# Higher scheduling priority for the chain from the output projection to the first MLP input tiles, and row scalings on VectorE, in a decoder layer on one core

## The chip, the core and the metric

The kernel runs on one core of a Trainium2 chip. TensorE (PE) does the matrix products and the transposes, VectorE (DVE) and ScalarE (ACT) work on rows of 128 partitions, GpSimd (POOL) does a few small operations, SyncE (SP) issues the transfers between the memory of the chip and the core's SBUF. PSUM holds what TensorE writes. The metric is the device time of one execution in microseconds (us); the median of the runs counts.

## The reference

One decoder layer over 2048 tokens of width 1024, in float32. A conditioning vector gives six vectors (shift, scale and gate of each half of the layer), and every half normalises its input rows first:

```
mod = silu(c) @ w_ada + b_ada
sh1, sc1, ga1, sh2, sc2, ga2 = split(mod, 6)
h   = rms_norm(x, g_attn) * (1 + sc1) + sh1
z   = h @ w_in                      # both attention groups, one product
mix = concat(sliding_window(z), forgetting(z)) @ w_out
x   = x + ga1 * mix
h2  = rms_norm(x, g_mlp) * (1 + sc2) + sh2
u   = causal_conv3(h2 @ w_up)       # 2 * 2816 columns
a, g = split(u, 2)
x   = x + ga2 * ((silu(g) * a) @ w_down)
y   = rms_norm(x, g_final)
```

`rms_norm` multiplies each row by 1/sqrt(mean of its squares + eps). The sliding-window group looks at 128 keys, the forgetting group at all earlier ones, so its work grows with the position.

## The kernel before

The 2048 tokens are cut into four blocks of 512, each in four tiles of 128 rows (t0 to t3) by two halves of 512 columns. Every float32 product is made of three TensorE products of a high part and a low part: ScalarE casts the high part (`hh`, `wh`, `ph`, `yh`), VectorE subtracts it from the whole (`hl`, `wl`, `pl`, `yl`).

A block goes through three stages. s1 normalises its rows, transposes them and multiplies by `w_in`. s2 is the attention, here mostly that of the forgetting group: scores `s` in PSUM, bias on ScalarE into `t` (L973), running maximum `mx` and the sum `acc` on VectorE, the maximum subtracted (L1002, L1006), exponential on ScalarE (L1007), split into `ph` and `pl` (L716, L717), product with the values into `o` (L1051, L1054); small transposes (`mt`, `lt`, `mb`) carry the row maxima and sums. s3 is the output projection (L1171), the rest of the layer's first half, and the MLP (its up-projection is L1289). In time: s1 of block 0; s1 of blocks 1 and 2 beside the attention of block 0; then s3 of block 0 beside the attention of block 1, s3 of block 1 with s1 of block 3 beside the attention of block 2, s3 of block 2 beside the attention of block 3, and s3 of block 3 alone. The two streams of a stage are merged in the order in which the program is written.

The place that the change touches lies in s3 between the output projection and the up-projection; each block passes it once. For each tile t and each half of the columns: VectorE multiplies the projection `d` by the gate into `gtmp` (L1245) and adds it to the residual row `x1row` (L1247); SP stores the row (L1248); ScalarE squares it and sums the squares into `ss` (`sumsq`, L487). After the second half: POOL makes `rs` = (sum + eps)^-0.5 in two instructions (L491, L492), and ScalarE scales the first half of the row in place (`pscale`, L114) and the second half into `gtmp` (L1255). Then `lazy_h` makes the input tiles of the MLP one by one, in two parts of 256 tokens (t0 and t1, then t2 and t3): TensorE transposes 128x128 pieces of the scaled rows into `d` (L513), ScalarE applies scale and shift (`hraw`, L521, with `scl` and `mod`) and casts `hh` (L114), VectorE subtracts `hl` (L526). The first block's own rows go the same way at the very start (`prep_tile`, rows `xrow`, tiles `xt`, first product L278), beside the first part of `mod` (L201 and L203 on VectorE, summed over partitions by L258 on TensorE, finished by L263 to L265).

What sets the order: a tile scheduler takes the whole program, keeps a priority for each instruction (by default the order in which it was written) and writes a fixed order for each engine; at run time an engine takes its instructions in that order and waits at the head of its queue. VectorE's and SP's order at the start is written out by hand, and is kept.

## Time and profile before

| | |
|---|---|
| median of 3 runs | 2670.57 us (2666.57 to 2671.02) |
| the profiled execution | 2663.14 us, its span 2661.4 us, mean granted TensorE clock 0.976 of full |
| TensorE busy | 2544.1 us, 96% of the span |
| VectorE, ScalarE, GpSimd busy | 1918.8 us (72%), 1472.0 us (55%), 91.7 us (3%) |

The profiled execution lies 7.43 us under the median of the timed runs. Busy time of TensorE contains matmuls whose ends are modelled, so what matters is where it has no work at all, and the stretches in which its clock is below full.

### The profile page before, as it was taken

To read this page: it belongs to the slowest core of one execution; us is meant where nothing else is said; L and a number is where in the kernel's file an instruction comes from. 1 tells how busy PE (TensorE), PEld (TensorE's weight loads), DVE (VectorE), ACT (ScalarE), POOL (GpSimd) and SP (SyncE) were. 2 spreads that over 40 slices of the span, in tenths; PEclk is the share of its full clock that TensorE was granted. 3 is DMA by queue.
4 is the path that set the end of the run, shared out by engine and by line. 5 is a ranking of instruction groups with operands and counts; after the bars stand their busy time and mean duration, and the time that the engine had idled before them with its cause. 6 is when DMAs were issued, how large, how long until landed. Compare 5 with 4: busy or idle time off the path is not lost.

```text
span 2661.4 us, 38402 instructions
## 1 busy us (share of the span) xinstructions
PE 2544.1 (96%) x12852; PEld 2155.2 (81%) x12852; DVE 1918.8 (72%) x3813; ACT 1472.0 (55%) x3085; POOL 91.7 (3%) x171
## 2 busy tenths in 40 slices
PE   7999989799999999989999999799998999999998
PEld 5888888688887889878888888688877878888887
DVE  5568767799998668778888767888888876344433
ACT  4456665655667675575556665755555665421222
POOL 1001000100000010010000000100000000000000
PEclk9999999799999999999999999899998999999999
DMA  6967679576557876756666799365554577655564
GB/s 229 303 204 256 194 226 339 179 257 212 183 188 216 284 253 213 254 184 234 227 231 235 256 304 315 100 216 193 185 168 142 173 238 236 227 197 191 190 236 175
DMA packets 304769, 588.24 MB, mean 221 GB/s; under 512 B 32188, under 2 KB 137396, under 8 KB 304572
## 3 DMA queue, kind: packets, MB, share of 16 engines
q1 hardware_dynamic: 304572, 585.79, 65.8%
q8 instruction: 102, 1.67, 0.3%
q14 instruction: 95, 0.78, 0.1%
HBM read 440.95 MB, written 144.71 MB: 220 GB/s over the span
## 4 chain that ended last, share of the span: by engine, by line
PE 83%; DVE 5%; DMA 5%; ACT 4%; issue 2%; POOL 1%; SPq 1%; POOLq 0%; DVEq 0%; ACTq 0%
PE d L1289 36%; PE d L1171 21%; PE d L611 8%; PE s L956 4%; PE d L639 3%; PE o L1054 2%; PE o L1051 2%; PE d L278 1%; PE mb L988 1%; DVE t L1002 1%; PE s L786 1%; DMA yraw<-yd 1%; DMA q<-qd 1%; DMA wada<-in_w_ada_dram 1%; PE pt L828 1%
## 5 line engine op out<-in xcount | busy, mean ns | idle before, releaser
L1289 PE MATMUL d<-hh,wkh 128*128 128x512 f32 (+1 forms) x920 | 352.9, 386 | 13.4 <-DVE halo L1333 8.7
L1289 PE MATMUL d<-hl,wkh 128*128 128x512 f32 (+1 forms) x920 | 353.7, 386 | 0.0
L1289 PE MATMUL d<-hh,wkl 128*128 128x512 f32 (+1 forms) x920 | 352.5, 384 | 0.0
L381 DVE TENSOR_TENSOR wl<-wr,wh 128x1024 fp32r<-128x1024 f32 (+5 forms) x184 | 218.9, 1190 | 84.1 <-ACT wh L380 82.1
L973 ACT ACTIVATE t<-s,bc 128x256 f32<-128x256 f32 (+3 forms) x464 | 201.1, 483 | 135.7 <-PE s L956 72.0
L380 ACT CAST wh<-wr 128x1024 fp32r<-128x1024 f32 (+5 forms) x184 | 188.7, 1026 | 152.0 <-PE d L1289 62.8
L1319 ACT ACTIVATE u<-d,cb,cw 128x512 f32<-128x512 f32 x176 | 136.3, 777 | 207.7 <-PE d L1289 190.8
L716 ACT CAST ph<-t 128x512 fp32r<-128x512 f32 (+2 forms) x304 | 176.8, 590 | 119.3 <-PE o L1051 117.8
L1322 DVE SCALAR_TENSOR_TENSOR u<-d,cw,u 128x511 f32<-128x511 f32 x176 | 130.4, 743 | 150.7 <-ACT u L1319 149.6
L717 DVE TENSOR_TENSOR pl<-t,ph 128x512 fp32r<-128x512 f32 (+2 forms) x304 | 192.5, 644 | 31.5 <-ACT ph L716 31.2
L1289 PE MATMUL d<-hl,wh 128*128 128x512 f32 (+1 forms) x552 | 211.9, 385 | 0.0
L1289 PE MATMUL d<-hh,wh 128*128 128x512 f32 (+1 forms) x552 | 211.2, 384 | 0.4 <-ACT hh L114 0.4
L1289 PEld LDWEIGHTS d<-hh,wkh 128*128 128x128 f32 x920 | 173.9, 190 | 46.5 <-DVE halo L1333 9.3
L1289 PE MATMUL d<-hh,wl 128*128 128x512 f32 (+1 forms) x552 | 210.9, 383 | 0.0
L956 PE MATMUL s<-q,kkb 128*128 128x256 f32 (+2 forms) x1024 | 195.1, 309 | 7.3 <-ACT t L973 3.1
L1289 PEld LDWEIGHTS d<-hh,wkl 128*128 128x128 f32 x920 | 174.9, 190 | 32.0
L1289 PEld LDWEIGHTS d<-hl,wkh 128*128 128x128 f32 x920 | 174.9, 190 | 31.3 <-DVE hl L526 0.2
L1007 ACT ACTIVATE t<-t 128x512 f32<-128x512 f32 (+2 forms) x304 | 170.2, 601 | 13.0 <-DVE t L1006 10.1
L956 PEld LDWEIGHTS s<-q,kkb 128*128 128x128 f32 x1024 | 152.0, 194 | 19.9 <-ACT t L973 5.3
L1051 PE MATMUL o<-ph,vvb 128*128 128x256 f32 (+2 forms) x512 | 150.8, 310 | 10.0 <-ACT ph L716 3.6
L1054 PE MATMUL o<-pl,vvb 128*128 128x256 f32 (+2 forms) x512 | 146.7, 306 | 8.7 <-DVE pl L717 8.7
L611 PE MATMUL d<-hh,wh 128*128 128x512 f32 x360 | 142.0, 398 | 5.5 <-DVE lf L654 3.9
(232 smaller groups left out, 6078.9 us busy)
## 6 DMA issues: line engine op xcount, KB each, us to landing
wkh<-wsu SPq DMA_DIRECT2D x110, 512.0 KB, 3.3
wkl<-wsu SPq DMA_DIRECT2D x110, 512.0 KB, 4.2
wr<-in_w_up_dram SPq DMA_DIRECT2D x66, 512.0 KB, 4.8
wkh<-wsd SPq DMA_DIRECT2D x55, 512.0 KB, 3.9
wkl<-wsd SPq DMA_DIRECT2D x55, 512.0 KB, 4.3
wada<-in_w_ada_dram SPq DMA_DIRECT2D x96, 256.0 KB, 5.5
wr<-in_w_in_c_dram SPq DMA_DIRECT2D x45, 512.0 KB, 4.3
wsu<-wh SPq DMA_DIRECT2D x44, 512.0 KB, 2.9
```

The costliest lines, as they stand in the source:

```text
L380: nc.scalar.copy(wh, raw)
L381: nc.vector.tensor_sub(wl, raw, r32(wh))
L611: nc.tensor.matmul(ps, a[:, k, :], b[k], start=(k == 0 and i == 0), stop=(k == KT - 1 and i == 2),)
L716: nc.scalar.copy(ph[:, e0:], src[:, e0:])
L717: nc.vector.tensor_sub(pl[:, e0:], src[:, e0:], r32(ph[:, e0:]))
L956: nc.tensor.matmul(ps[:, o + low(c0) : o + w], st["kks"][kb // 4][:, (kb % 4) * P : (kb % 4 + 1) * P], qs[a][:, low(c0) : w], start=(a == ...
L973: nc.scalar.activation(tt[:, plain : o + w], ps[:, plain : o + w], AF.Identity, bias=bias(kb))
L1007: nc.scalar.activation(t1, t1, AF.Exp)
L1051: nc.tensor.matmul(po[:, c:], v, ph[:, o + c : o + w], start=(kb == 0), stop=False)
L1054: nc.tensor.matmul(po[:, c:], v, pl[:, o + c : o + w], start=False, stop=(kb == nkb - 1))
L1171: nc.tensor.matmul(acc[t], l[:, ts], r[:, k % 2, :], start=(i == 0 and l is ah and r is wh), stop=(i == n_k - 1 and l is al),)
L1289: nc.tensor.matmul(ps[:, c], w[a][:, k, :], b[k][:, c], start=(k == 0 and i == 0), stop=(k == KT - 1 and i == 2),)
```

## The change

A scheduling context `first()` raises the priority of what is written inside it by 400 places. It is put around the second half's loop over the four tiles (gate, add, sums, `rsqrt`, scalings) and around the making of the MLP's input tiles (`lazy_h` with two parts). Inside the loop the scaling of the first half of a row goes from ScalarE to VectorE, and the store of the row is written behind the sums. At the start the eight scalings of the first block's rows go from ScalarE to VectorE. 24 instructions change their engine in all (8 at the start, 4 for each block). Lines behind the new function are 4 further down than before, those behind the loop 8 further.

```diff
+AHEAD = 400
...
+    def first():
+        return tc.high_priority(offset=AHEAD)
...
                 j = made[part]
-                a, b = h_pair(hh, hl, j)
-                ps = side_ps(w) if side else dense_ps(w)
-                transposes(ps, rows[part * nt : (part + 1) * nt], j)
-                modulate_one(a[:, c], b[:, c], ps, j, a0, s0)
+                with first() if parts == 2 else nullcontext():
+                    a, b = h_pair(hh, hl, j)
+                    ps = side_ps(w) if side else dense_ps(w)
+                    transposes(ps, rows[part * nt : (part + 1) * nt], j)
+                    modulate_one(a[:, c], b[:, c], ps, j, a0, s0)
...
         rs = rms(row)
         for r in row:
-            pscale(r, r, rs)
+            if n == 0:
+                nc.vector.tensor_scalar(r, r, rs, None, ALU.mult)
+            else:
+                pscale(r, r, rs)
...
-                tmp = tp.tile([P, 512], F32, tag="t", name="gtmp")
-                row = rows[t][half]
-                nc.vector.tensor_mul(tmp, r[t], gb)
-                adder = nc.vector
-                adder.tensor_add(row, row, tmp)
-                nc.sync.dma_start(x1_d[n][t * P : (t + 1) * P, cs], row)
-                if half == 0:
-                    sss.append(sums())
-                sumsq(row, sss[t][:, half : half + 1], tmp)
-                if half == 1:
-                    rs = rsqrt(sss[t])
-                    pscale(rows[t][0], rows[t][0], rs)
-                    nc.scalar.activation(tmp, row, AF.Copy, scale=rs)
-                    rows[t][1] = tmp
+                with first() if half == 1 else nullcontext():
+                    tmp = tp.tile([P, 512], F32, tag="t", name="gtmp")
+                    row = rows[t][half]
+                    nc.vector.tensor_mul(tmp, r[t], gb)
+                    nc.vector.tensor_add(row, row, tmp)
+                    if half == 0:
+                        sss.append(sums())
+                    sumsq(row, sss[t][:, half : half + 1], tmp)
+                    nc.sync.dma_start(x1_d[n][t * P : (t + 1) * P, cs], row)
+                    if half == 1:
+                        rs = rsqrt(sss[t])
+                        nc.vector.tensor_scalar(rows[t][0], rows[t][0], rs, None, ALU.mult)
+                        nc.scalar.activation(tmp, row, AF.Copy, scale=rs)
+                        rows[t][1] = tmp
```

What the scheduler makes of it shows in the orders of the engines. The orders before and after agree outside the start, the four places between projection and up-projection, and one long stretch: from block 2's place on, through the attention of block 3, nearly every engine's order is another one. POOL's order is unchanged, SP's changes in a few rows.

VectorE in block 1, beside the attention, before. L1247 are the adds of t2 and t3, L1002 the subtraction of the maximum, L1032 and L1036 the reciprocal `rl` of the attention's sums:

```order
L1247 TENSOR_TENSOR x1row<-x1row,gtmp 128x512
L1002 TENSOR_TENSOR t<-t,mm 128x512 x6
L933 TENSOR_TENSOR mx<-t 128x512
L378 TENSOR_TENSOR wl<-wr,wh 128x512
L1245 TENSOR_TENSOR gtmp<-d,gb_12125 128x512
L378 TENSOR_TENSOR wl<-wr,wh 128x512
L1032 TENSOR_REDUCE rl<-lt 128x2
L1014 TENSOR_TENSOR acc<-t 128x512
L1247 TENSOR_TENSOR x1row<-x1row,gtmp 128x512
L939 TENSOR_TENSOR mx<-mx,t 128x512
L1036 RECIPROCAL rl<-rl 128x2
```

The same place of the changed kernel, from the add of t2 on:

```order
L1255 TENSOR_TENSOR x1row<-x1row,gtmp 128x512
L1010 TENSOR_TENSOR t<-t,mm 128x512 x6
L1262 TENSOR_SCALAR x1row<-x1row,rs 128x512
L941 TENSOR_TENSOR mx<-t 128x512
L382 TENSOR_TENSOR wl<-wr,wh 128x512
L1254 TENSOR_TENSOR gtmp<-d,gb_12125 128x512
L382 TENSOR_TENSOR wl<-wr,wh 128x512
L1040 TENSOR_REDUCE rl<-lt 128x2
L1262 TENSOR_SCALAR x1row<-x1row,rs 128x512
L1022 TENSOR_TENSOR acc<-t 128x512
L947 TENSOR_TENSOR mx<-mx,t 128x512
L1255 TENSOR_TENSOR x1row<-x1row,gtmp 128x512
```

The six subtractions still stand ahead of t3's gate and add; two scalings (of t1 and t2) have come in between, and t0's stands a few rows ahead of the first row shown.

TensorE in block 2, beside the attention, before. L956 are scores, L1051 and L1054 products with the values, L513 the transposes of the scaled rows:

```order
L988 MATMUL mb<-ident,rl 128x128 x2
L956 MATMUL s<-q,kkb 128x256 x4
L1051 MATMUL o<-ph,vvb 128x256
L513 MATMUL d<-ident,x1row 128x128 x3
L1054 MATMUL o<-pl,vvb 128x256
L1051 MATMUL o<-ph,vvb 128x256
```

In the changed kernel the same `mb` products and four score products are followed by L1059 and L1062, six of each in turn, and then:

```order
L1059 MATMUL o<-ph,vvb 128x256
L1062 MATMUL o<-pl,vvb 128x256
L964 MATMUL s<-q,kkb 128x256 x8
L517 MATMUL d<-ident,x1row 128x128 x6
L964 MATMUL s<-q,kkb 128x256 x4
```

Eleven value products and eight score products that stood behind the first transposes now stand ahead of them, and the six transposes of the first part stand together.

ScalarE in block 3, with no attention beside it, before. L487 are the sums of squares (the first row holds four of the first half of the columns and that of t0), L114 on `x1row` and L1255 the two scalings of a row, L521 and L114 on `hraw` the input tiles:

```order
L487 ACTIVATE gtmp,ss<-x1row 128x512 x5
L114 ACTIVATE x1row<-x1row,rs 128x512
L1255 ACTIVATE gtmp<-x1row,rs 128x512
L487 ACTIVATE gtmp,ss<-x1row 128x512 x2
L114 ACTIVATE x1row<-x1row,rs 128x512
L1255 ACTIVATE gtmp<-x1row,rs 128x512
L114 ACTIVATE x1row<-x1row,rs 128x512
L1255 ACTIVATE gtmp<-x1row,rs 128x512
L521 ACTIVATE hraw<-d,mod,scl 128x256 x3
L487 ACTIVATE gtmp,ss<-x1row 128x512
L114 ACTIVATE hh<-hraw 128x256 x3
```

And in the changed kernel:

```order
L491 ACTIVATE gtmp,ss<-x1row 128x512 x5
L1263 ACTIVATE gtmp<-x1row,rs 128x512
L491 ACTIVATE gtmp,ss<-x1row 128x512
L1263 ACTIVATE gtmp<-x1row,rs 128x512
L491 ACTIVATE gtmp,ss<-x1row 128x512
L525 ACTIVATE hraw<-d,mod,scl 128x256 x3
L115 ACTIVATE hh<-hraw 128x256
L491 ACTIVATE gtmp,ss<-x1row 128x512
L1263 ACTIVATE gtmp<-x1row,rs 128x512
```

The first three `hraw` stand behind the scaling of t1 and no longer behind the scalings of t2, and the scalings of `x1row` are gone from ScalarE.

## Rows read from the trace of the kernel before

**Rows 1.** TensorE's waits: for which line, us in total, times, longest.

```profile
PE d L513 <- ACT x1row L114: 14.5, 4, 7.6
PE sd L513 <- ACT xrow L114: 10.0, 4, 6.3
```

**Rows 2.** Stretches: busy time by engine, granted clock (PEclk), DMA share.

```profile
0.00:30.00 30.00, 12.80 (x49) 10.33 (x50) 14.35 (x31) 21.65 (x42) 6.82 (x19) 1.00 0.92 330
...
1133.00:1180.00 47.00, 38.51 (x243) 34.60 (x242) 39.64 (x79) 40.92 (x96) 11.33 (x10) 0.89 0.49 158
1660.00:1720.00 60.00, 45.26 (x292) 39.92 (x291) 47.97 (x91) 46.41 (x109) 7.99 (x10) 0.89 0.32 104
1720.00:2240.00 520.00, 495.01 (x2589) 420.35 (x2588) 424.73 (x883) 310.44 (x699) 2.46 (x12) 0.97 0.56 187
2274.00:2310.00 36.00, 31.60 (x189) 28.70 (x188) 13.51 (x27) 22.61 (x50) 3.64 (x8) 0.91 0.39 139
```

**Rows 3.** Durations of two forms: ns min/median/max, first and last start.

```profile
L114 ACT ACTIVATE x1row<-x1row,rs x16: 704/722/735, 478.1 to 2288.1; 128x512 f32<-128x512 f32 x16
L201 DVE TENSOR_SCALAR acc<-wada,cc x12: 457/482/487, 11.8 to 570.5; 128x512 f32<-128x512 f32 x12
```

**Rows 4.** Timeline of the start: start us, length us, instruction, idle before.

```profile
16.03 1.34 ACT L114 ACTIVATE xrow<-xrow,rs 128x512 f32<-128x512 f32 x2 [0.83 <-POOL rs L492]
...
12.46 5.47 DVE L203 SCALAR_TENSOR_TENSOR acc<-wada,cc,acc 128x512 f32<-128x512 f32 x7 [0.19 <-DMA wada<-in_w_ada_dram]
20.82 1.23 DVE L381 TENSOR_TENSOR wl<-wr,wh 128x1024 fp32r<-128x1024 f32 x1 [2.89 <-ACT wh L380]
...
25.32 0.16 DVE L265 SCALAR_TENSOR_TENSOR scl<-mod,gat 128x2 f32<-128x2 f32 x1
...
27.67 2.08 PE L278 MATMUL d<-hh,wh 128*128 128x512 f32 x4 [4.54 <-ACT hh L114]
```

**Rows 5.** Timeline of block 0's place.

```profile
507.75 1.22 PE L956 MATMUL s<-q,kkb 128*128 128x512 f32 x2 [2.99 <-DVE mod L215]
```

**Rows 6.** Timeline of block 1's place.

```profile
1148.42 0.15 DVE L1036 RECIPROCAL rl<-rl 128x2 f32<-128x2 f32 x1
...
1152.67 0.63 ACT L487 ACTIVATE gtmp<-x1row 128x512 f32<-128x512 f32 x1
...
1148.72 0.40 PE L988 MATMUL mb<-ident,rl 128*128 128x128 f32 x2 [3.83 <-DVE rl L1036]
...
1161.58 1.14 PE L513 MATMUL d<-ident,gtmp 128*128 128x128 f32 x4 [3.21 <-ACT hraw L521]
...
1153.49 5.57 POOL L491 TENSOR_SCALAR rs<-ss 128x1 f32<-128x1 f32 x1 [2.47 <-ACT gtmp L487]
1159.14 0.57 POOL L492 TENSOR_TENSOR rs<-rs,mhalf 128x1 f32<-128x1 f32 x1
```

**Rows 7.** Timeline of block 2's place.

```profile
1680.12 1.88 DVE L717 TENSOR_TENSOR pl<-t,ph 128x512 fp32r<-128x512 f32 x3
...
1679.00 4.02 POOL L491 TENSOR_SCALAR rs<-ss 128x1 f32<-128x1 f32 x1 [21.47 <-ACT gtmp L487]
...
1684.90 0.90 PE L513 MATMUL d<-ident,x1row 128*128 128x128 f32 x3 [7.61 <-ACT x1row L114]
1685.45 0.56 PE L1054 MATMUL o<-pl,vvb 128*128 128x256 f32 x1
...
1687.73 0.41 PE L1054 MATMUL o<-pl,vvb 128*128 128x256 f32 x1
```

**Rows 8.** Timeline of block 3's place.

```profile
2282.24 0.72 ACT L114 ACTIVATE x1row<-x1row,rs 128x512 f32<-128x512 f32 x1
...
2284.82 1.47 ACT L521 ACTIVATE hraw<-d,mod,scl 128x256 f32<-128x256 f32 x3
...
2287.26 0.58 PE L1289 MATMUL d<-hh,wkh 128*128 128x256 f32 x1 [3.70 <-ACT hh L114]
...
2278.17 0.30 POOL L491 TENSOR_SCALAR rs<-ss 128x1 f32<-128x1 f32 x1 [30.45 <-ACT gtmp L487]
```

## The prediction

> **What bounds the kernel now.** Start with the table: TensorE is busy for 2544.1 of 2661.4 us, so all that a reordering can win is some 117 us of idle time and the stretches with a reduced clock. TensorE's waits [rows 1] say how much of that belongs to the scaled rows: 14.5 us in four waits at the places between projection and up-projection, 10.0 us in four waits at the start. The stretches [rows 2] show the same places as the ones where TensorE is idle and its clock falls: 0.89 of full (on average between the two levels, 1.2 and 2.4 GHz) around blocks 1 and 2, 0.91 around block 3, against 0.97 in the long stretch beside the last attention. The timelines of the places [rows 4 to 8] then tell which wait ends last there, and it is not the same one each time. A place is left behind by TensorE at most once, so what is won there stays won if TensorE is the bound behind it; I read that from 495.01 busy of 520 us in the long stretch [rows 2].
>
> **The moved instructions.** A scaling of 128x512 takes 0.72 us on ScalarE and 0.48 us on VectorE in its like [rows 3]. ScalarE and VectorE are at 55% and 72% in the table, so the 24 moved instructions (11.5 us on VectorE) count only where something waits behind them. The store of the rows comes later in the code; SP's order hardly moves, and nothing at these places waits for it, so it costs nothing; were that cover gone, it would be one sum of squares, 0.63 us [rows 6], for each tile.
>
> **The start.** The last tile's two scalings begin at 16.03 and take 1.34 us, after 0.83 us of waiting for `rs` [rows 4]. In the changed kernel ScalarE does only sums, so the sums of the last tile no longer stand behind the scalings of two other tiles (2 x 1.34, nearly 2.5 us with overlap); VectorE does the last pair in 2 x 0.48; rows are ready about 3.5 us earlier, near 13.8 instead of 17.4. But the eight scalings stand ahead of the adaLN sums on VectorE: these now end at 12.46 + 5.47 = 17.93, and after the change at 13.8 + 0.48 + 5.47 = 19.8. From there VectorE has the work that lies between 20.82 and 25.32 [rows 4], 4.5 us with gaps of up to 1 us that an earlier ScalarE fills, so `scl` comes at 23.4 to 24.3 in place of 25.3, and the first product with it (27.67 now, after 4.54 us idle). I take -1.8. Bounds: 0 if the weights are not there earlier (the DMA share is 0.92 in these 30 us [rows 2]), -3.5 if the rows alone count, +1.9 if the late sums do.
>
> **Block 0.** The wait that ends last here is not for a scaled row: TensorE waits 2.99 us at 507.75 for `mod`, which VectorE finishes behind its adaLN sums [rows 5]. Rows that come earlier run into that wait. Four scalings are added to VectorE's queue ahead of it, 4 x 0.48 = 1.9 us, part of it in VectorE's own idle time. I take +0.8, with bounds -1 and +1.9.
>
> **Block 1.** Here the chain does end last: t3's sums of squares start on ScalarE at 1152.67, POOL's first instruction begins at 1153.49 and takes 5.57 us, the second ends at 1159.71; TensorE then waits 3.21 us for `hraw` at 1161.58 [rows 6]. In block 3, where VectorE is idle meanwhile, the same first instruction takes 0.30 us [rows 8]. So POOL was held up while VectorE ran subtractions without a pause. In the new order VectorE has a scaling in its queue that needs this `rs`, so it must stop and lets POOL through: `rs` about 1.5 us behind its sums, near 1155, some 5 us sooner. The 3.21 us go. Of the clock (47 us at 0.89 are 5.2 us of full speed lost [rows 2]) I take a quarter, 1.3. Against it, three scalings come ahead of the reciprocal at 1148.42, for which TensorE already waits 3.83 us [rows 6]: 3 x 0.48 = +1.4. Sum -3.1; bounds -6 (both idle stretches' clock comes back) and +1.5 (only the delay).
>
> The Trainium skill has a rule for POOL's long instruction: "SBUF — State Buffer", section "Who interferes with whom", says that VectorE and GpSimd share a pair of ports as an exclusive lock, which VectorE takes with two operands in SBUF against a GpSimd read, and with a `tensor_scalar` in a two-port mode. The trace agrees in the first half: 5.57 us against 0.30 us beside two-operand subtractions. The second half speaks against this change, since the moved scalings are `tensor_scalar`; by it the sum would be a little smaller (the rival of the scalings, below).
>
> **Block 2.** TensorE's longest wait of this kind is 7.61 us until 1684.90, for the row, whose `rs` came out of a POOL instruction of 4.02 us from 1679.00 [rows 7]. VectorE's adds stay behind the subtractions, so the sums start almost as before. Two things move. VectorE stops at t0's scaling after the three splits that end at 1682.0 [rows 7], so POOL is through near 1683.1 and the row at 1683.6, 1.3 us earlier. And eleven value products that now run from 1685.45 to about 1688 [rows 7], some 2.5 us, stand ahead of the transposes in the new order; their splits are ready from 1680.7 to 1682.0, so they fill the wait. -2.5 - 1.3 = -3.8, the moved scores not counted. Bounds: -7.6 (the whole wait) and 0. The late one next is ScalarE, whose bias and casts for the attention queue up with `hraw`; if that ends last, the wait is only handed on.
>
> **Block 3.** No attention runs beside it, and everything is the chain. Between 2282.24 and 2284.82 ScalarE does four scalings (2.58 us) before the first `hraw`, and TensorE waits 3.70 us for the first `hh` at 2287.26 [rows 8]. In the new order one of the four and one sum remain: 2 x 0.62 less, 1.3 us; and the first `hh` no longer stands behind a sum, 0.6 us. With a third of the 3.2 us that a clock of 0.91 costs over 36 us [rows 2], 1.1: -3.0. Bounds -1.3 and -4.8.
>
> **The long stretch.** From 1720 to 2240 nearly every order is another one. TensorE is idle for 520 - 495.01 = 25.0 us there [rows 2]. Nothing in the trace of before says which way a new order goes: I take 0, and a quarter of that idle time, 6 us, both ways.
>
> **Sum.** -1.8 + 0.8 - 3.1 - 3.8 - 3.0 = -10.9 us. Against the profiled execution that is 2663.14 - 10.9 = 2652.2 us. It lies 7.43 us under the median of the runs, so I predict 2652.2 + 7.43 = 2659.7, rounded 2660 us.
>
> **The rivals.**
> Given back: the waits at the places shrink, but the attention beside them ends last (ScalarE in block 2, `mod` in block 0), and the new order of the long stretch returns some. For it: TensorE's 25.0 us idle there with no single cause, and the share of the 14.5 us that block 0 cannot use. Against: block 3 has no such partner. Only the start and half of block 3 remain, -3.3, and half of the stretch's 6 us is lost: 2670.57 - 0.3 = 2670 us. Chance 0.16.
>
> Scalings against POOL: each scaling on VectorE holds up the `rs` of the next tile by its own length, 0.48 us, three times in each of four places: +5.8, so 2659.7 + 5.8 = 2665.5 us. For it: the 5.57 us [rows 6]. Against: the scaling waits for the previous `rs`, so POOL has mostly begun. Chance 0.08. It is what the rule of the Trainium skill's page named above would do here.
>
> Slower: VectorE stops at each scaling with the attention's splits, maxima and reciprocals queued behind it, and TensorE waits for those. Price of one stop: `rs` 0.30 + 0.57 [rows 6, 8] plus 0.48, or 1.35 us; twelve scalings beside attention, 16.2 us. With the gains of blocks 1 and 2 lost and start and block 3 kept, -4.8 + 16.2 = +11.4, 2682 us. It decides from 0.9 us for each scaling on (10.9 / 12). For it: the reciprocal at 1148.42, for which TensorE waits. Against: VectorE has 28% idle. Chance 0.16.
>
> More: the whole of the 7.61, 3.21 and 3.70 us, with the clock of these places: 4 us more in block 2, 3 in block 1, 2 in block 3, 1.7 at the start, 2649 us. Chance 0.10. That leaves 0.50 for my forecast, 2650 to 2665 us.
>
> **How the numbers follow.** Less than 0.2%, 5.3 us, can't be told from no change on this kernel: faster is below 2665.2 us, slower above 2675.9. Forecast and "more" are faster, 0.60; given back and the scalings against POOL the same, 0.24; the slower rival 0.16. The terms' bounds (some 3 us in blocks 1 and 2, 1.5 at the start and in block 3, 6 in the stretch) give about 8 us as roots of squares; the likeliest case alone is 2651 to 2668. For 8 in 10 I go up to the given-back case and part of the slower one: 2648 to 2675.
>
> **What would show it.** Start: first product near 26 instead of 27.67. Block 1: POOL's instruction for t3 under 2 us, no wait near 3 us for `hraw`; the wait for the reciprocal longer than 3.83. Block 2: eleven value products ahead of the transposes, in a wait that was empty, and the up-projection's start about 4 us earlier against the projection's end. Block 3: first up-projection 2 us earlier against the projection's end, and the clock back sooner. Wrong I would be if TensorE's waits for `pl` (VectorE) grow by more than 5 us in sum, if the row's wait in block 2 stays at 7 us, or if TensorE's idle time in the long stretch moves by more than 6 us.

## The result, and the profile after

The changed kernel takes 2653.11 us (median of 4 runs, 2650.55 to 2654.82) where the kernel before takes 2668.57 us on the same chip (2665.91 to 2671.02): a ratio of 0.9942, with an interval of 0.9927 to 0.9956, or 15.5 us less. Measured a second time, beside other runs of before, the ratio was 0.9951 (0.9936 to 0.9965). The two profiled executions lie closer together, 2663.14 and 2654.82 us; where that comes from is found below with the second profile of before.

TensorE's busy time is almost the same (2544.1 us before); what went is for the most part idle time. First the page's busy line, then TensorE's waits, of the changed kernel:

```profile
PE 2542.7 (96%) x12852; PEld 2152.4 (81%) x12852; DVE 1927.9 (73%) x3837; ACT 1457.2 (55%) x3061; POOL 86.1 (3%) x171
```

```profile
PE o L1062 <- DVE pl L725: 19.2, 18, 3.4
...
PE sd L517 <- DVE xrow L568: 6.5, 4, 4.8
...
PE mb L996 <- ACT ph L724: 5.2, 1, 5.2
...
PE d L1297 <- ACT hh L115: 3.0, 3, 2.1
```

The wait for `x1row` of 14.5 us [rows 1] is gone altogether. Something stands in its place: TensorE now waits 19.2 us for `pl`, the low parts that VectorE splits off. The difference is where the time is spent. A transposed row was waited for with nothing else to do; the waits for `pl` are many and short.

The same stretches as in [rows 2], moved to where the places lie now (a window of equal length around the same work):

```profile
1134.00:1181.00 47.00, 41.43 (x280) 38.31 (x279) 41.52 (x84) 39.50 (x92) 6.69 (x10) 0.93 0.47 159
1657.00:1717.00 60.00, 48.61 (x312) 42.92 (x311) 48.47 (x95) 44.43 (x102) 8.40 (x9) 0.91 0.30 100
2267.00:2303.00 36.00, 33.18 (x193) 29.59 (x193) 16.13 (x35) 20.29 (x47) 3.98 (x8) 0.91 0.43 161
1717.00:2233.00 516.00, 490.48 (x2568) 415.83 (x2567) 426.36 (x885) 309.06 (x701) 2.66 (x13) 0.98 0.57 189
```

TensorE is busy for 2.9 us longer in the window of block 1, 3.4 us longer in that of block 2, 1.6 us longer in that of block 3. The granted clock rose in block 1 (0.89 to 0.93) and block 2 (0.89 to 0.91), and did not in block 3, where it is 0.91 as before.

The timelines of the places, changed kernel, in the order start, block 0, block 1, block 2, block 3 (each line: start, length, instruction, idle before):

```profile
12.91 0.88 DVE L568 TENSOR_SCALAR xrow<-xrow,rs 128x512 f32<-128x512 f32 x2 [0.90 <-POOL rs L496]
...
14.22 5.47 DVE L207 SCALAR_TENSOR_TENSOR acc<-wada,cc,acc 128x512 f32<-128x512 f32 x7
...
23.32 0.16 DVE L269 SCALAR_TENSOR_TENSOR scl<-mod,gat 128x2 f32<-128x2 f32 x1
...
25.67 2.08 PE L282 MATMUL d<-hh,wh 128*128 128x512 f32 x4 [3.99 <-ACT hh L115]
...
510.10 1.22 PE L964 MATMUL s<-q,kkb 128*128 128x512 f32 x2 [2.74 <-DVE mod L219]
...
1150.72 0.16 DVE L1044 RECIPROCAL rl<-rl 128x2 f32<-128x2 f32 x1
...
1151.02 0.66 PE L996 MATMUL mb<-ident,rl 128*128 128x128 f32 x2 [5.16 <-ACT ph L724]
...
1153.18 1.81 POOL L495 TENSOR_SCALAR rs<-ss 128x1 f32<-128x1 f32 x1 [2.12 <-ACT gtmp L491]
1155.07 0.81 POOL L496 TENSOR_TENSOR rs<-rs,mhalf 128x1 f32<-128x1 f32 x1
...
1154.71 0.40 DVE L1070 TENSOR_TENSOR yo<-yo,mb 64x256 f32<-64x256 f32 x1
...
1155.92 0.49 DVE L1262 TENSOR_SCALAR x1row<-x1row,rs 128x512 f32<-128x512 f32 x1 [0.47 <-POOL rs L496]
...
1675.15 3.69 POOL L495 TENSOR_SCALAR rs<-ss 128x1 f32<-128x1 f32 x1 [20.95 <-ACT gtmp L491]
...
1679.58 0.59 POOL L495 TENSOR_SCALAR rs<-ss 128x1 f32<-128x1 f32 x1
...
1679.52 0.49 DVE L1262 TENSOR_SCALAR x1row<-x1row,rs 128x512 f32<-128x512 f32 x1 [0.53 <-POOL rs L496]
...
1677.51 0.58 PE L1062 MATMUL o<-pl,vvb 128*128 128x256 f32 x1 [2.97 <-DVE pl L725]
...
1679.81 0.42 PE L1062 MATMUL o<-pl,vvb 128*128 128x256 f32 x1
...
1682.85 0.74 PE L964 MATMUL s<-q,kkb 128*128 128x256 f32 x4 [1.77 <-ACT t L981]
1683.42 0.82 PE L517 MATMUL d<-ident,x1row 128*128 128x128 f32 x6
...
2277.76 0.39 PE L1297 MATMUL d<-hh,wkh 128*128 128x256 f32 x1 [2.10 <-ACT hh L115]
```

Start: the rows are ready at 13.8 us, the adaLN sums end at 19.7, `scl` comes at 23.3, the first product at 25.67 in place of 27.67 [rows 4]. Block 0: the wait for `mod` is still there, 2.74 in place of 2.99 us [rows 5]. Block 1: `rs` of t3 ends at 1155.88 in place of 1159.71 [rows 6], there is no wait for `hraw`, and the wait ahead of `rl` has grown from 3.83 to 5.16 us. Block 2: eleven value products run from 1677.51 to 1680.0 in the wait that was empty for 7.61 us [rows 7], ahead of the six transposes; TensorE now waits 2.97 us for `pl` ahead of them and 1.77 us for ScalarE's `t` behind them. Block 3: the first up-projection waits 2.10 us in place of 3.70 [rows 8].

To compare kernels place by place, the text below uses one measure: TensorE runs 12852 matmuls in each of them, so the time between two matmuls, counted in order of their start, is the time that a place took, wherever it lies. Block 0 is matmul 2200 to 2480, block 1 5480 to 5800, block 2 8180 to 8420, the long stretch 8420 to 11100, block 3 11100 to 11300. These are us in one profiled execution each, with the time ahead of block 0 (0 to 2200) in the first column; the experiments that the rows name follow:

```
                          to block 0  block 0  block 1  block 2  stretch  block 3
before                        446.65    76.17    61.76    50.23   541.46    40.78
before, again          (e1)   444.89    75.25    60.87    51.97   542.77    40.34
start only             (e2)   441.77    75.94    59.71    50.35   546.01    39.97
priority only          (e3)   445.86    73.23    60.47    51.87   546.11    40.00
scalings only          (e4)   444.84    77.39    57.30    47.46   540.02    37.98
stop on VectorE        (e5)   448.64    75.83    58.09    48.98   539.79    39.97
first halves unscaled  (e6)   445.51    76.17    60.32    44.19   540.03    39.45
both halves            (e7)   449.55    78.88    57.17    45.21   544.75    35.81
start and scalings     (e8)   444.81    75.85    57.31    47.46   542.02    39.63
after                         449.18    75.97    56.59    47.46   540.28    39.84
after, again           (e9)   444.88    76.10    56.60    47.45   540.19    39.05
both, last block       (e10)  444.40    78.53    57.31    47.45   542.22    35.80
both, blocks 2 and 3   (e11)  444.27    75.33    57.31    45.97   544.38    35.82
start; both, 2 and 3   (e12)  444.33    77.69    57.33    45.95   544.87    35.82
```

This measure has a weakness where TensorE's order changes: the same count need not mean the same work. By matmul 8420 the changed kernel has done ten up-projection products of 512 columns and ten of 256 more than the kernel before, and twenty attention products of 256 columns fewer. Its block 2 therefore holds more work than that of before, and its long stretch less. At 5800 (e4, e7, e8, e10 to e12) and at 11300 (e7, e10 to e12) two products differ. The second table goes by counts by which every kernel has done the same number of products of each kind: block 1 from 5480 to 5945, block 2 from 8180 to 8470 (e11 and e12 differ from the others there, so their first comparable count is 9173), the stretch from 8470 to 11100, block 3 from 11100 to 11400.

```
                          block 1  block 2  8180-9173  9173-11100  stretch  block 3
before                      93.29    59.56     193.57      398.12   532.13    61.61
before, again          (e1) 92.40    61.29     195.30      399.43   533.44    61.17
start only             (e2) 91.24    59.68     193.69      402.67   536.68    60.79
priority only          (e3) 92.00    61.15     195.36      402.63   536.83    60.81
scalings only          (e4) 89.05    55.74     190.42      397.06   531.74    58.79
stop on VectorE        (e5) 89.62    58.31     192.32      396.45   530.46    60.80
first halves unscaled  (e6) 91.85    52.69     187.43      396.80   531.53    60.26
both halves            (e7) 88.00    54.00     192.29      397.67   535.96    56.85
start and scalings     (e8) 89.06    55.74     190.43      399.05   533.74    60.47
after                       88.16    55.71     190.41      397.32   532.03    60.65
after, again           (e9) 88.18    55.70     190.41      397.23   531.94    59.86
both, last block      (e10) 89.06    55.73     190.43      399.25   533.94    56.85
both, blocks 2 and 3  (e11) 89.06        -     193.56      396.79        -    56.86
start; both, 2 and 3  (e12) 89.08        -     193.55      397.27        -    56.86
```

Times given with the experiments are of the first table, as the expectations are, where nothing else is said.

### The profile page after: what moved, and what is told of

Read it like the earlier page. It is cut to its first block, busy times and chain, and to the rows that moved or that the text cites. A ratio compares the mean times of both kernels' runs of the same rounds, so it can differ in the third digit from the quotient of the medians.

```text
span 2653.1 us, 38432 instructions
## 1 busy us (share of the span) xinstructions
PE 2542.7 (96%) x12852; PEld 2152.4 (81%) x12852; DVE 1927.9 (73%) x3837; ACT 1457.2 (55%) x3061; POOL 86.1 (3%) x171
## 4 chain that ended last, share of the span: by engine, by line
PE 83%; DVE 6%; DMA 5%; ACT 3%; issue 1%; SPq 1%; POOL 1%; POOLq 0%; DVEq 0%; ACTq 0%
PE d L1297 36%; PE d L1179 21%; PE d L619 8%; PE s L964 4%; PE d L647 3%; PE o L1062 2%; PE o L1059 2%; PE d L282 1%; PE s L794 1%; PE mb L996 1%; PE pt L836 1%; DVE t L1010 1%; DMA zrow<-zd 1%; DMA wr<-in_w_in_c_dram 1%; DMA wada<-in_w_ada_dram 1%
## 5 line engine op out<-in xcount | busy, mean ns | idle before, releaser
L1015 ACT ACTIVATE t<-t 128x512 f32<-128x512 f32 (+2 forms) x304 | 170.0, 602 | 15.5 <-DVE t L1014 11.6
L1062 PE MATMUL o<-pl,vvb 128*128 128x256 f32 (+2 forms) x512 | 147.0, 306 | 19.4 <-DVE pl L725 19.2
L1059 PE MATMUL o<-ph,vvb 128*128 128x256 f32 (+2 forms) x512 | 150.1, 309 | 11.7 <-ACT ph L724 5.6
```

Of the source, the lines that this page charges most:

```text
L1015: nc.scalar.activation(t1, t1, AF.Exp)
L1059: nc.tensor.matmul(po[:, c:], v, ph[:, o + c : o + w], start=(kb == 0), stop=False)
L1062: nc.tensor.matmul(po[:, c:], v, pl[:, o + c : o + w], start=False, stop=(kb == nkb - 1))
```

## The experiments

My theory going in: the gain comes from the places, because VectorE's stop at the scaling lets POOL through (blocks 1 and 2), because value products fill the wait (block 2), and because ScalarE has less to do (block 3); the start's gain is lost again. The rivals: the raised priority alone does it; ScalarE's relief alone does it; the start carries what the places don't.

**e1, the kernel before again** (no edit).

> The kernel before, a second time, so that a second profile of it can be laid beside the first, stage by stage. Theory (the places between projection and up-projection give the gain, and the start's gain is spent waiting for weights): the profile agrees with the first one within 0.3 us at each of the four places, and moves by some us only in stretches with the DMA share near 1 (before 130 us and around 340 to 400 us). Rival (the profiled execution of before was a lucky one at the places, which would explain why the runs differ by 15 us and the profiles by 8): the places move by 2 us or more. Time: 1.000 of before, within 0.002.

Ratio 0.9994 (0.9981 to 1.0006). The theory's part of this was too neat: the places moved by 0.4 to 1.7 us between two executions of the same program, not by 0.3, and the largest move, 3.7 us, lies between matmul 5800 and 8180. POOL's long instruction of block 1 is there to the hundredth:

```profile
1149.75 5.57 POOL L491 TENSOR_SCALAR rs<-ss 128x1 f32<-128x1 f32 x1 [2.47 <-ACT gtmp L487]
```

In e2, the next kernel, it took 4.38 us, and block 1 took 59.71 us: there the scheduler had put one small reduction of VectorE (`rl<-lt`) ahead of a maximum, and VectorE came to a pause at it.

The second pair of profiles, e1 and e9, lies 13.0 us apart (2664.78 and 2651.77 us), the first pair 8.3. Of the 4.7 us between these two differences, 2.5 lie ahead of block 0, where the first profile of after was slow (449.18 us, in e9 444.88), and 3.1 between matmul 8180 and 11100, where the first profile of before was quick (591.7 us, in e1 594.7); the rest cancels. Between 5800 and 8180 both first profiles were quick (473.6 and 474.5 us, then 477.2 and 477.5), so that stretch explains nothing of it.

**e2, the start only.**

```diff
-            pscale(r, r, rs)
+            if n == 0:
+                nc.vector.tensor_scalar(r, r, rs, None, ALU.mult)
+            else:
+                pscale(r, r, rs)
```

> Only the eight scalings of the first block's rows go to VectorE; nothing else of the change. Theory: the first product comes 2 us earlier (near 25.7 instead of 27.67), and this is spent before 130 us in waits for the third weight group, so the time stays within 0.1%: 2667 to 2671 us beside 2668.6. Rival (the start carries the half of the gain that the places don't explain): 0.2 to 0.3% faster, 2661 to 2663 us.

Ratio 0.9996 (0.9982 to 1.0011): no difference that can be told, as the theory said. But its reason falls. The first product is early,

```profile
26.10 2.08 PE L278 MATMUL d<-hh,wh 128*128 128x512 f32 x4 [4.19 <-ACT hh L114]
```

and in this profile the lead is still 2.0 us at the 500th matmul; it is not spent in waits for weights by then. Over all profiles the first product stands at 26.2 us with the new start (25.67 to 26.88, five) and at 27.5 us with the old one (26.59 to 28.13, nine), so 1.3 us is won there. At matmul 2200 the two groups are at 445.0 and 446.1 us, but single executions lie between 441.8 and 449.2 in the one and 444.3 and 449.6 in the other. What the start is worth lies between 0 and some 2 us, and stays open.

**e3, the priority only**: the changed kernel without its start, and with

```diff
-                        nc.vector.tensor_scalar(rows[t][0], rows[t][0], rs, None, ALU.mult)
+                        pscale(rows[t][0], rows[t][0], rs)
```

> Only the raised priority of both pieces; all scalings stay on ScalarE, and the start is that of before. Theory (VectorE's stop at the scaling lets POOL through, and ScalarE's relief gives block 3): POOL's instruction for t3 in block 1 stays above 3 us, blocks 1 and 3 gain less than 1.5 us each, block 2 keeps its 3 us from the products that stand ahead: 3 to 5 us faster in all, ratio 0.998 to 0.999. Rival (the order alone does it): ratio 0.994 to 0.996, with gains at all three places like those of the whole change.

Ratio 1.001 (0.9997 to 1.0023): no gain, where I expected a small one. In block 1 `rs` of t3 still needs 4.91 us on POOL (before: 5.57 and 0.57, 6.14 in all), shared out between the two instructions:

```profile
1148.06 2.00 POOL L495 TENSOR_SCALAR rs<-ss 128x1 f32<-128x1 f32 x1 [2.85 <-ACT gtmp L491]
1150.14 2.91 POOL L496 TENSOR_TENSOR rs<-rs,mhalf 128x1 f32<-128x1 f32 x1
```

In block 2 the first transposes stay where they were in TensorE's order, behind one value product, and the place takes 51.87 us. So the eleven products ahead of the transposes are not the priority's work; the next kernel shows whose they are.

**e4, the scalings of x1row only**: the kernel before with

```diff
-                    pscale(rows[t][0], rows[t][0], rs)
+                    nc.vector.tensor_scalar(rows[t][0], rows[t][0], rs, None, ALU.mult)
```

> Only the scaling of the first half of each x1row goes to VectorE, with the old priorities; the start is that of before. Theory: POOL is let through in block 1 (its instruction for t3 under 2 us) and ScalarE is relieved, so blocks 1 and 3 gain 2 to 4 us each, block 2 nothing: ratio 0.997 to 0.998. Rival (the order alone does it): within 0.1%. Second rival (VectorE stops with the attention's work behind it): slower by 0.1 to 0.4%.

Ratio 0.9955 (0.9938 to 0.9972): one line alone gives what the whole change gives, as far as these intervals tell. That is more than I expected: block 2, for which I had nothing, gains as well. Blocks 1, 2 and 3 take 57.30, 47.46 and 37.98 us. TensorE's order in block 2 has the value products and scores ahead of the transposes, with the old priorities: the scheduler moved them when the scaling changed its engine. POOL's instruction in block 1 (2.37 us, where I had said under 2), and what VectorE did at its end (the last line is the scaling that waits):

```profile
1150.59 2.37 POOL L491 TENSOR_SCALAR rs<-ss 128x1 f32<-128x1 f32 x1 [2.12 <-ACT gtmp L487]
```

```profile
1152.13 0.74 DVE L526 TENSOR_TENSOR hl<-hraw,hh 128x256 fp32r<-128x256 f32 x2
1153.65 0.48 DVE L1254 TENSOR_SCALAR x1row<-x1row,rs 128x512 f32<-128x512 f32 x1 [0.78 <-POOL rs L492]
```

VectorE's last operation ends at 1152.87, POOL's first instruction at 1152.96.

**e5, a stop without relief**: the kernel before with a small instruction on VectorE that reads `rs`.

```diff
+                    seen_rs = sp.tile([P, 1], F32, tag="rsd", name="rsd")
+                    nc.vector.tensor_scalar(seen_rs, rs, 1.0, None, ALU.mult)
                     pscale(rows[t][0], rows[t][0], rs)
```

> The kernel before, with one more small instruction on VectorE (a 128x1 copy of rs, read by nobody) at the place in the program where the scaling would be; both scalings stay on ScalarE. It makes VectorE stop for rs without relieving ScalarE. Theory (the stop lets POOL through, which is what blocks 1 and 2 need): POOL's instruction for t3 in block 1 under 2.5 us and that of block 2 near 3.2 us, block 1 gains 3 us or more, block 2 1 us, block 3 nothing: ratio 0.998 to 0.999. Rival (ScalarE's relief is what counts): block 1 gains under 1 us, ratio within 0.1% of 1.

Ratio 0.9979 (0.9968 to 0.9989). A useless instruction makes the kernel faster by 0.2%, through the wait that it brings:

```profile
1154.10 1.43 POOL L491 TENSOR_SCALAR rs<-ss 128x1 f32<-128x1 f32 x1 [2.35 <-ACT gtmp L487]
...
1679.37 3.17 POOL L491 TENSOR_SCALAR rs<-ss 128x1 f32<-128x1 f32 x1 [21.47 <-ACT gtmp L487]
```

```profile
1154.95 0.41 DVE L526 TENSOR_TENSOR hl<-hraw,hh 128x256 fp32r<-128x256 f32 x1
1156.21 0.15 DVE L1255 TENSOR_SCALAR rsd<-rs 128x1 f32<-128x1 f32 x1 [0.86 <-POOL rs L492]
```

Block 1 takes 58.09 us, 3.2 less than the mean of 61.3 us in the two profiles of before; block 2 48.98, 2.1 less than 51.1; block 3 39.97, where before has 40.34 and 40.78 and e2 39.97. That is the theory's picture, with more in block 2 than I said. The scheduler also moved a few instructions near the new one (on ScalarE the two scalings of the row, by two places), so not all of the gain need be the stop's; POOL's times are. In block 2 POOL's instruction ended at 1682.54, while VectorE still ran its last operation ahead of the stop (1682.30 to 1682.70).

**e6, relief without a stop**: the kernel before without the line

```diff
-                    pscale(rows[t][0], rows[t][0], rs)
```

> The kernel before without the scaling of the first half of each x1row (left out, so those rows go into the MLP unscaled). It relieves ScalarE without giving VectorE a stop. Theory (POOL must be let through in blocks 1 and 2, ScalarE's relief is for block 3): POOL's instruction for t3 in block 1 stays at 4 us or more and block 1 gains under 2 us, block 3 gains 2 to 3 us: ratio 0.998 to 0.999. Rival (ScalarE's relief is all): block 1 gains 4 us or more as with the scalings on VectorE, ratio 0.994 to 0.997.

Ratio 0.9958 (0.9944 to 0.9972), like the rival's, but not for the rival's reason. Block 1 gains 1.0 us only, and POOL is still held up, if a little less than the 4 us I had said:

```profile
1149.70 3.70 POOL L491 TENSOR_SCALAR rs<-ss 128x1 f32<-128x1 f32 x1 [2.93 <-ACT gtmp L487]
```

The gain is in block 2, 52.69 us by the second table, 7.7 less than the mean of 60.43 of before: rows that need no scaling don't wait for `rs`, so the first transposes could be placed ahead of everything. In block 3 ScalarE's relief alone is worth 1.1 us, not the 2 to 3 that I expected.

**e7, both halves on VectorE**: e4 and, for the second half,

```diff
-                    nc.scalar.activation(tmp, row, AF.Copy, scale=rs)
+                    nc.vector.tensor_scalar(tmp, row, rs, None, ALU.mult)
```

> Scalings of both halves of each x1row on VectorE, old priorities, old start. Theory: VectorE has 0.48 us more per tile in front of the attention's splits, ScalarE 0.72 us less; block 3 gains about 1 us more than with one half, blocks 1 and 2 lose as much; ratio like that of the first halves alone, 0.994 to 0.997. Rival (VectorE becomes the late engine): 0.998 or more, with TensorE's waits for the splits up by 5 us.

Ratio 0.9965 (0.9951 to 0.9979). By the second table block 3 takes 56.85 us, 4.5 less than the 61.39 of before, a far larger gain than I expected; block 2 takes 54.00, against 55.74 in e4. From matmul 8470 to 9173, directly behind, e7 gives 3.6 us back (138.3 us, e4 134.7). Block 0 took 78.88 us, but kernels with e4's block 0 took 75.33 to 78.53, so a loss there is not shown. TensorE's waits for the splits were no longer than with first halves alone (e7, then e4), so VectorE did not become the late engine.

```profile
PE o L1054 <- DVE pl L717: 15.2, 12, 3.8
```

```profile
PE o L1054 <- DVE pl L717: 14.9, 10, 3.8
```

**e8, start and scalings, no priority**: e2 and e4 together.

> Everything of the change but the raised priority: scalings of the first block and of the first halves of x1row on VectorE, old priorities. Theory (the priority adds nothing): 0.994 to 0.997, like the whole change. Rival (the priority gives a part of its own): 0.998 or more.

Ratio 0.997 (0.996 to 0.9981), at the edge of what the theory allowed. The places are e4's in blocks 1 and 2. Beside e4's 0.9955 it says that the start adds nothing that these runs can tell. About the priority it says more than I had expected: e8 is the changed kernel without it, and its interval does not meet that of the changed kernel's first measurement (0.9942, 0.9927 to 0.9956) and touches that of the second (0.9951, 0.9936 to 0.9965). On top of the scalings the priority may thus be worth some 0.2%, though it was worth nothing alone (e3). The profiles show 0.9 us of it, in block 1: 88.16 and 88.18 us in the two profiles of the whole change, 89.05 to 89.08 in the five kernels with first halves on VectorE and the old priorities. The rest is not found at any place, and e4, without priority and start, is level with the whole change; what the priority adds stays open.

**e9, the changed kernel again** (no edit).

> The changed kernel a second time, for a second profile and for runs beside the next two kernels. Theory: the places agree with the first profile of after within 1 us (block 1 56.6 us, block 2 47.5 us, block 3 39.8 us between the same two matmuls), block 3 up to 2 us less if the clock comes back sooner; ratio 0.994 to 0.996. Rival (the first result was partly luck of the long stretch): ratio 0.996 to 0.998.

Ratio 0.9951 (0.9936 to 0.9965). Blocks 1 and 2 repeat to 0.01 us (56.60, 47.45), block 3 takes 39.05.

**e10, both halves in the last block alone**, and **e11, in blocks 2 and 3**: e4 and

```diff
-                    nc.scalar.activation(tmp, row, AF.Copy, scale=rs)
+                    if n == NB - 1:
+                        nc.vector.tensor_scalar(tmp, row, rs, None, ALU.mult)
+                    else:
+                        nc.scalar.activation(tmp, row, AF.Copy, scale=rs)
```

with `n >= 2` in e11.

> First halves of x1row on VectorE in all blocks, second halves too in the last block alone; old priorities and start. Theory (ScalarE is what is late in block 3, and a shorter wait there leaves TensorE at 2.4 GHz): block 3 takes near 36 us where the first halves alone take 38 to 39.6, the other places as with the first halves alone; ratio 0.993 to 0.996. Rival (block 3's 35.8 us came from the other order of the long stretch): 38 us or more.

> As the kernel with both halves in the last block, and both halves on VectorE in block 2 as well. Theory: block 2 takes near 45 us in place of 47.5, block 3 near 36, and the long stretch keeps its 540 to 542 us: ratio 0.992 to 0.995, the best version of these. Rival (the new order of the long stretch takes it back, as where both halves moved in all blocks): the stretch near 545 us, ratio 0.995 to 0.997.

Ratios 0.9963 (0.9946 to 0.9979) and 0.9949 (0.9933 to 0.9966). Block 3 took 35.80 and 35.82 us, so it is the last block's own edit and not the order ahead of it; e10's ratio is just past the bound that I had given. In e10 the wait for the first up-projection (timeline), and the stretch around block 3 (as in [rows 2]), are:

```profile
2280.37 0.39 PE L1292 MATMUL d<-hh,wkh 128*128 128x256 f32 x1 [1.71 <-ACT hh L114]
```

```profile
2268.00:2304.00 36.00, 34.21 (x210) 30.05 (x209) 19.18 (x41) 19.21 (x44) 3.58 (x8) 1.00 0.53 188
```

TensorE's clock stays at its upper level, 2.4 GHz, through the whole place. In e11 block 2 takes 45.97 us, near the expected 45, and the long stretch 544.38 us, which its rival had said. Part of both is the cut: at matmul 8420 e11 has done thirty-one attention products fewer than the kernel before, and thirty-one products of the up-projection more. From 8180 to 9173, with equal work, e11 takes 193.56 us where e4 and e10 take 190.4, so the second halves on VectorE lose 3.1 us in block 2 or right behind it; from 9173 on e11 takes 396.79 us, among the least. The sum is no better than the whole change's.

**e12, the start as well**: e2 and e11 together.

> The first block's scalings and the first halves of x1row on VectorE, second halves too in blocks 2 and 3; old priorities. Theory (the start gives 1 to 2 us at most, the places add up): blocks 1 to 3 take near 57.3, 46.0 and 35.8 us, ratio 0.993 to 0.996, the best version or level with it. Rival (the parts undo each other in the order of the long stretch): the stretch at 544 us or more and a ratio above 0.996.

Ratio 0.9963 (0.9946 to 0.998). The places are as expected by the first table (57.33, 45.95, 35.82) and the stretch is the rival's, 544.87 us; the second table shows e11's loss from 8180 to 9173 again (193.55 us). The ratio is just past the theory's bound, and its interval holds both. No version was found that beats the changed kernel by more than the runs can tell; e11 comes level with it.

## Why the prediction was right, step by step

The forecast, 2660 us in a range of 2648 to 2675, was 10.9 us less than before. Measured were 15.5 and, the second time, 0.49% or 13.1 us. By places, with equal work (second table; block 0 from the first), the mean of the two profiles of before (before, e1) against that of the two of after:

| term | forecast | measured |
|---|---|---|
| start | -1.8 | -1.3 at the first product; 0 to -2 at block 0, open |
| block 0 | +0.8 | 75.71 to 76.04, +0.3 |
| block 1 | -3.1 | 92.85 to 88.17, -4.7 |
| block 2 | -3.8 | 60.43 to 55.70, -4.7 |
| block 3 | -3.0 | 61.39 to 60.26, -1.1 |
| long stretch | 0 | 532.79 to 531.99, -0.8, open |

The sum came nearer than its parts, and that is luck: block 3 gave 1.9 us less than forecast, blocks 1 and 2 together 2.5 more.

**Block 0** did what the forecast said: the wait that ends last there is the one for `mod`, and rows that are earlier run into it.

**Block 1** was right in its core, a little small, and the mechanism is shown beside the changed kernel rather than in it. That a pause of VectorE lets POOL through is shown by e5, whose edit adds nothing but the stop and wins 3.2 us, and by e6, which has the relief without the stop and wins 1.0. In block 1 POOL's first instruction ends 0.1 to 0.2 us after VectorE's last operation ahead of the stop in e4 and e5. So it does in e2 and e6, where VectorE came to a pause for another reason. In e2 it waited for TensorE's `lt` (the first line is POOL's, the others VectorE's):

```profile
1147.55 4.38 POOL L491 TENSOR_SCALAR rs<-ss 128x1 f32<-128x1 f32 x1 [2.47 <-ACT gtmp L487]
...
1151.08 0.68 DVE L720 TENSOR_TENSOR pl<-t,ph 128x512 fp32r<-128x512 f32 x1
1152.18 0.42 DVE L1035 TENSOR_REDUCE rl<-lt 128x2 f32<-128x256 f32 x1 [0.42 <-PE lt L1030]
```

In the changed kernel itself a pause is not what released the first instruction: it ends at 1154.99, 0.28 us into `yo<-yo,mb`, while VectorE is busy until 1155.45, and the stop of 0.47 us covers the second instruction. So a pause is one way through and not the only one. The forecast also misread its short case: in block 3 VectorE was not idle when POOL took 0.30 us from 2278.17 on, it was in the product with the gate (first line; the second is a `yo<-yo,mb` of block 2, both of the kernel before):

```profile
2277.94 0.69 DVE L1245 TENSOR_TENSOR gtmp<-d,gb 128x512 f32<-128x512 f32 x1 [0.62 <-PE d L1171]
...
1681.93 0.40 DVE L1062 TENSOR_TENSOR yo<-yo,mb 64x256 f32<-64x256 f32 x1
```

Both operations read one input from PSUM (`d`, `mb`), where eleven of the fourteen operations beside the 5.57 us (six subtractions, the rest sums and maxima) read both inputs from SBUF. That this is what counts is not shown: beside that `yo<-yo,mb` POOL stayed held, until 1683.02. How much of the changed kernel's gain in block 1 is the stop's own thus stays open.

The wait ahead of `rl` grew by 1.3 us, as priced (1.4); the profile puts its end down to ScalarE's `ph`, which came 0.1 us behind `rl`. The clock, for which I took 1.3 us, gave more: 0.93 over 47 us loses 3.3 us where 0.89 lost 5.2.

**Block 2** came as forecast, through the eleven value products in the empty wait. The warning that the wait is handed on came true in part: TensorE no longer waits for the row, but 1.77 us for ScalarE's `t` at 1682.85. Whose doing the new order is, the forecast left out, and the name of the change points to the wrong part: e3 has the priority and not the products, e4 has the products and not the priority. Of the rule from "SBUF — State Buffer" ("Who interferes with whom") in the Trainium skill, the half against the change can be seen here too: the `rs` of the next tile took 0.59 us at 1679.58, beside a scaling that began at 1679.52, against 0.30 us in block 3 [rows 8]. That is 0.3 us, less than the 0.48 of that rival, and TensorE did not wait for it.

**Block 3** was mis-sized. The idle part is right: in the window around the place TensorE is idle for 2.8 us (36 - 33.18) in place of 4.4 [rows 2], 1.6 us less where I had 1.9. The step that failed is "a third of the 3.2 us that a clock of 0.91 costs": the clock stayed at 0.91, and part of the idle time came back as slow products, so 1.1 us is left. e10 shows the other side: with the wait at 1.71 us the clock is 1.00, and with equal work the place takes 56.85 us where the changed kernel takes 60.65 and 59.86. Against the second profile of after that is 3.0 us. A clock of 0.91 over 36 us loses 3.2, so the clock alone covers it; TensorE's idle time in the two windows differs by 0.4 (busy for 34.21 us in e10, 33.81 in the second profile of after). The row of the second profile of after is

```profile
2263.00:2299.00 36.00, 33.81 (x196) 30.35 (x195) 15.18 (x31) 19.74 (x47) 3.98 (x8) 0.91 0.45 165
```

e4 lies between the two, with a wait of 2.10 us and the place at 58.79:

```profile
2264.00:2300.00 36.00, 33.42 (x202) 29.72 (x201) 15.72 (x33) 20.29 (x47) 3.98 (x8) 0.95 0.51 192
```

The length of this wait does not settle the clock by itself: e5 kept the old wait of 3.70 us and has 0.95 as well. What decides how far the clock falls here stays open.

```profile
2271.50:2307.50 36.00, 31.58 (x193) 28.11 (x192) 14.67 (x33) 23.39 (x51) 3.65 (x8) 0.95 0.45 167
```

**The start** came as priced at its own place (-1.3 for -1.8). That it is kept until block 0 was an assumption, "a place is left behind by TensorE at most once"; neither e2's time nor the profiles can say.

**The long stretch** was forecast at nothing, with 6 us both ways. With equal work the two profiles of after stand at 531.9 and 532.0 us; before, e1 and e5, whose order there is the old one, at 530.5 to 533.4. So the new order neither won nor lost there by anything that these profiles can tell; e4 and e8, with the same places, differ by 2.0. TensorE's idle time there hardly moved, from 25.0 us to 25.5 (516 - 490.48).

**The rivals.** Given back: no; only e7, e11 and e12 lose something, in block 2 or right behind it. Slower by stops on VectorE: no; VectorE did stop at the scalings, for 6.4 us in nine of the sixteen in the first profile of after, 0.4 us a scaling where that rival needed 0.9. TensorE's waits for `pl` grew from 8.7 us (12 waits, of before) to 19.2, which I had named as a sign that I would be wrong. First VectorE's waits of after (for what, us in total, times, longest), then the row for `pl` of before:

```profile
DVE x1row L1262 <- POOL rs L496: 6.4, 9, 1.2
```

```profile
PE o L1054 <- DVE pl L717: 8.7, 12, 1.4
```

The sign misled. Of the 10.5 us more, 4.7 lie in block 0, which took no longer for it (76.04 us for 75.71); 3.0 lie in block 2, where the products now run in time that was idle before; and 3.1 lie in the long stretch, where TensorE's idle time as a whole stayed.

## What to carry to other kernels

A run of one engine's operations without a pause can hold up another one's tiny instruction for microseconds (here VectorE's, for 4 to 5.6 us); look for a short instruction with a long time in the trace, and at what its neighbour does meanwhile. A work item moved to the engine that does the holding up can cure it, since it brings that engine to a stop where it must wait. When a change has two parts, test them apart and one on top of the other: here the priority did nothing alone, one line of the rest gave as much as the whole, and what the first adds on top of the second is still open. And before times between two counts are compared, see that the same work lies between them.

## What the runs showed that I had not expected

An instruction that does nothing but wait, 0.15 us on VectorE for each tile, made the kernel 0.2% faster (e5). The new places repeat to a few hundredths of a us across kernels (block 2: 55.70 to 55.74 in five profiles, block 3 with both halves 56.85 to 56.86 in four), while the same program varied by 1.8 and 4.3 us ahead of block 0, where the DMA share is high at the start [rows 2], and by 3.7 and 3.0 us between matmul 5800 and 8180. And 0.4 us less of waiting for the first up-projection, 1.71 us where it was 2.10, went with a granted clock of 1.00 in place of 0.91 to 0.95 over the 36 us around it, though 3.70 us of waiting went with 0.95 in e5.
